# Moving the gate, merge, mLSTM-input and output-projection products of a hybrid recurrent decoder step from fp32r parts to scaled fp16 parts

## The chip, the cores and the metric

The kernel runs on one core of one Trainium2 chip. The metric is the device time of one execution in microseconds. The kernel before has a median of 1895.54 us over three runs (1894.94 to 1898.8). Engines: TensorE (PE, its weight loads shown as PEld), VectorE (DVE), ScalarE (ACT), GpSimd (POOL) and SyncE (SP), which issues most weight loads.

## The reference

One layer of a decoder trunk over 288 tokens (256 of a prompt, 8 x 4 of samples), model width 2048. With `xn = rmsnorm(x) * (1 + sc1) + sh1`:

```
proj = xn @ w_in                      # 2048 x 12320: RG-LRU, GLA, mLSTM inputs, gates
y_lru, y_gla, y_ml = three recurrent branches, each 1024 wide
gate = sigmoid(mg)                    # 3 x 2048 columns of proj
merged = gate0 * (y_lru @ w_br_lru) + gate1 * (y_gla @ w_br_gla) + gate2 * (y_ml @ w_br_ml)
x = x + gt1 * (merged @ w_out)
x = x + gt2 * (relu(norm2(x) @ w_ff1)**2 @ w_ff2)   # hidden width 8192
```

All in float32. The six shift, scale and gate vectors come from `silu(c) @ w_ada`. The branch states (a linear recurrence, a GLA state per head, an mLSTM matrix memory) are outputs too.

## The kernel before

Features lie on partitions and the 288 tokens along the free axis, so a weight tile of 128x128 is the stationary operand and a tile of 128x288 moves. A float32 product is made of three: high weight by high input, high by low, low by high, summed in one PSUM bank. The three branches, called side work below, run beside the weight streams, as generators that `run` advances by one step after each chunk of a stream. A chunk is 128x1024 weights, 512 KB, and makes 24 products.

Two kinds of stream exist. `stream` (lines 159 to 169) loads a chunk into one of three raw buffers on SyncE's queue, ScalarE rounds it to an fp32r high part (line 160), VectorE subtracts to get the low part (line 162), and line 169 multiplies. Everything ahead of the feed-forward goes through it: q, k, v and the RG-LRU input in four rounds of four k-tiles each, then the GLA gate, then for each of the three branches four pairs of a merge-gate block and a merge block (`merge`), with the mLSTM input blocks ahead of the second branch and its output gate ahead of the third, then `wout`. The branch outputs are split into fp32r parts by `split` (lines 647 and 648).

`Block` (lines 224 to 264) is the fp16 form, used by the feed-forward alone. ScalarE squares each of the four chunks of a block with an accumulated row sum (`scan`, line 236), a small product with ones adds the partitions (`total`, line 240), VectorE turns the sum into a power of two (`power_of_two`, lines 198 to 201) and `convert` writes scaled high and low fp16 parts into a pair buffer: the high part on ScalarE (line 249) or VectorE (line 251), the low part on VectorE (line 252). Line 263 multiplies. `feed_forward` scans ten chunks ahead, converts three ahead, and keeps the order of PE, ACT and DVE instructions of the stream as written (`in_order`). The order of the rest on each engine comes from the planner of the tile framework, by priorities; SyncE's order is the program's.

The conditioning products (`cond_product`, line 372, and `cond_parts`, line 433) are issued in between by a pattern of letters given to `every`.

## Time and profile before

| what | value |
|---|---|
| median of the runs | 1895.54 us |
| profiled execution | 1895.68 us |
| its span, first to last instruction | 1893.9 us |
| busy share PE / DVE / ACT / POOL | 98 / 67 / 59 / 12% |
| fp32r products (line 169) end, first fp16 product | 1084.8, 1093.8 us |
| granted TensorE clock | 0.995 |

A row of a group reads: line, engine, operation, output and inputs, shapes, count, then busy time and mean duration, then idle time ahead of it with what ended most of it. TensorE products overlap in the pipeline, so the length of one is not the distance between two. The chain of waits is read as start, length and what ran. A row of stages gives busy time and instruction count per engine.

### The profile page before, as it was taken

What the parts mean: (1) busy time and instruction counts of PE and PEld (TensorE: products, weight loads), DVE (VectorE), ACT (ScalarE), POOL (GpSimd) and SP (SyncE); (2) the same over time, 40 slices, a digit from 0 to 9 for tenths busy, and PEclk for the clock granted to TensorE, in tenths of its full rate; (3) what the DMA queues carried; (4) which work ended last, traced back from release to release, by engine and by line L of the source; (5) the groups of instructions that cost most, each with busy time, mean ns of one, the idle gap of its engine ahead of it and who ended that gap; (6) DMA issues with size and microseconds to landing.
All of it is one profiled execution on the core that took longest, in us unless ns stands there. A gap on an engine that the chain in (4) does not pass through costs nothing.

```text
span 1893.9 us, 38893 instructions
## 1 busy us (share of the span) xinstructions
PE 1847.8 (98%) x15874; PEld 1621.6 (86%) x15874; DVE 1268.2 (67%) x2239; ACT 1117.3 (59%) x1861; POOL 219.9 (12%) x302
## 2 busy tenths in 40 slices
PE   8999999999999999999999979999999999999997
PEld 7998889999999999999999947777777777777775
DVE  4767846645684557776558678776868676767676
ACT  5333374545454444566448568877777766666673
POOL 0001200000123010011101520000000000000091
PEclk9999999999999999999999999999999999999999
DMA  9998666547844358856787656565556555556541
GB/s 384 398 372 301 242 236 240 201 145 260 276 159 168 134 172 296 302 204 223 296 341 298 246 210 222 172 222 185 189 188 203 176 181 168 188 169 188 168 155 51
DMA packets 113442, 422.90 MB, mean 223 GB/s; under 512 B 11808, under 2 KB 12096, under 8 KB 110064
## 3 DMA queue, kind: packets, MB, share of 16 engines
q1 hardware_dynamic: 97040, 361.04, 54.9%
q0 software_dynamic: 11472, 42.79, 6.4%
q10 hardware_dynamic: 4752, 16.60, 2.2%
q8 instruction: 124, 2.03, 0.4%
q14 instruction: 54, 0.44, 0.1%
HBM read 403.56 MB, written 16.81 MB: 222 GB/s over the span
## 4 chain that ended last, share of the span: by engine, by line
PE 80%; DVE 9%; ACT 6%; issue 3%; DMA 1%; POOL 0%; SPq 0%; DVEq 0%; ACTq 0%; POOLq 0%
PE mm L169 39%; PE mm L263 24%; PE pi L263 6%; PE pa L372 3%; DVE pair L252 2%; ACT pair L249 2%; PE px L169 2%; DVE lo L162 1%; ACT con L236 1%; DMA raw<-win 1%; ACT hi L160 1%; PE pa L433 1%; DVE pair L251 0%; DVE s L800 0%; PE px L1649 0%
## 5 line engine op out<-in xcount | busy, mean ns | idle before, releaser
L263 PEld LDWEIGHTS <-pair 128*128 128x128 f16 x6144 | 596.6, 98 | 176.8 <-issue 11.9
L160 ACT ACTIVATE hi<-raw 128x1024 fp32r<-128x1024 f32 x272 | 286.9, 1057 | 407.4 <-PE mm L169 250.4
L162 DVE TENSOR_TENSOR lo<-raw,hi 128x1024 fp32r<-128x1024 f32 x272 | 334.9, 1233 | 248.0 <-ACT hi L160 227.9
L169 PE MATMUL mm<-xh,hi 128*128 128x288 f32 x1440 | 429.4, 301 | 4.0 <-ACT xh L718 1.7
L169 PE MATMUL mm<-xl,hi 128*128 128x288 f32 x1440 | 423.5, 297 | 0.0
L169 PE MATMUL mm<-xh,lo 128*128 128x288 f32 x1440 | 411.9, 296 | 2.0 <-DVE lo L162 1.9
L263 PE MATMUL mm<-x,pair 128*128 128x288 f16 x2448 | 316.1, 287 | 10.1 <-ACT x L1824 6.3
L263 PE MATMUL mm<-hx,pair 128*128 128x288 f16 x2472 | 321.8, 286 | 2.7 <-ACT s L1873 1.4
L169 PEld LDWEIGHTS mm<-xh,hi 128*128 128x128 f32 x1440 | 270.4, 188 | 15.8 <-issue 8.1
L169 PEld LDWEIGHTS mm<-xl,hi 128*128 128x128 f32 x1440 | 270.8, 188 | 1.4
L169 PEld LDWEIGHTS mm<-xh,lo 128*128 128x128 f32 x1440 | 266.0, 188 | 4.9 <-DVE lo L162 2.9
L169 PE MATMUL mm<-s,hi 128*128 128x288 f32 x1280 | 252.8, 297 | 1.1 <-DVE s L1769 0.7
L169 PEld LDWEIGHTS mm<-s,hi 128*128 128x128 f32 x1280 | 201.8, 188 | 5.1 <-issue 2.9
L169 PE MATMUL mm<-s,lo 128*128 128x288 f32 x640 | 179.2, 296 | 1.6 <-DVE lo L162 1.0
L252 DVE SCALAR_TENSOR_TENSOR pair<-xl,sums,pair 128x1024 f16<-128x1024 f32 x92 | 117.8, 1284 | 62.9 <-ACT pair L249 61.6
L252 DVE SCALAR_TENSOR_TENSOR pair<-s,sums,pair 128x1024 f16<-128x1024 f32 x92 | 118.1, 1284 | 52.7 <-ACT pair L249 51.4
L252 DVE SCALAR_TENSOR_TENSOR pair<-raw,sums,pair 128x1024 f16<-128x1024 f32 x72 | 93.2, 1295 | 41.6 <-ACT pair L249 40.6
L169 PEld LDWEIGHTS mm<-s,lo 128*128 128x128 f32 x640 | 116.9, 188 | 2.3 <-DVE lo L162 2.1
L1861 POOL TENSOR_SCALAR s<-s,mod 128x256 f32<-128x256 f32 x16 | 21.5, 1347 | 675.7 <-DVE s L1877 675.7
L236 ACT ACTIVATE con<-s 128x1024 bf16<-128x1024 f32 x92 | 96.3, 1046 | 1.3 <-DMA s<-wf 0.3
L236 ACT ACTIVATE con<-xl 128x1024 bf16<-128x1024 f32 x92 | 96.2, 1046 | 0.9
L263 PE MATMUL pi<-hx,pair 128*128 128x288 f16 x600 | 89.8, 286 | 3.1 <-DVE rs_t L1767 1.8
(526 smaller groups left out, 2275.7 us busy)
## 6 DMA issues: line engine op xcount, KB each, us to landing
raw<-win SPq DMA_DIRECT2D x192, 512.0 KB, 4.4
s<-wf SPq DMA_DIRECT2D x92, 512.0 KB, 3.9
xl<-wf SPq DMA_DIRECT2D x92, 512.0 KB, 4.1
raw<-wf SPq DMA_DIRECT2D x72, 512.0 KB, 3.9
s<-wq SPq DMA_DIRECT2D x20, 1024.0 KB, 8.7
raw<-wout SPq DMA_DIRECT2D x32, 512.0 KB, 5.9
s<-wada SPq DMA_DIRECT2D x13, 1024.0 KB, 7.3
ag<-wada POOLq DMA_DIRECT2D x12, 1024.0 KB, 7.8
```

The source lines that it names most:

```text
L160: pace["hi"] = S.activation(hi, raw, AF.Copy)
L162: pace["lo"] = V.tensor_tensor(out=lo, in0=raw, in1=hi.bitcast(F32), op=ALU.subtract)
L169: pace["last"] = T.matmul(ps, w[:, kk, ms], x, start=k == k0 and i == 0, stop=k == kt - 1 and i == 2)
L236: pace["hi"] = S.activation(junk, raw, AF.Square, accum_out=self.of[:, g:g + 1])
L249: pace["hi"] = S.activation(hi, raw, AF.Copy, scale=self.u)
L252: pace["lo"] = V.scalar_tensor_tensor(lo, raw, self.u, hi, ALU.mult, ALU.subtract)
L263: pace["last"] = T.matmul(self.ps[m][:, :N], a[:, kk, m * P:(m + 1) * P], x, start=k == 0 and i == 0, stop=k == 4 * self.kg - 1 and i == 2)
L372: pace["prod"] = T.matmul(ps[32 * j:32 * j + 32, h * w // 4:(h + 1) * w // 4], stat(k), v[:, j], start=k == 0 and h == 0, stop=k == kt - 1 ...
L433: pace["prod"] = T.matmul(ps[32 * j:32 * j + 32, a:a + 256], c, v[:, j], start=q == i == n == 0, stop=q == KT // each - 1 and n == 1, skip ...
L1861: G.tensor_scalar(a[:, 0:NP], a[:, 0:NP], mod[:, GT2, k, 0:1], None, ALU.mult)
```

## The change

The streams from the GLA gate to `wout` become `Block`s, in one list with the feed-forward's, fed by one pipeline (`feed`, `pipe_fetch`, `pipe_scan`, `pipe_total`, `pipe_convert`). Blocks of `win` beyond column 3072 (a new array `win2`) and of `wout` become 256 wide, four k-tiles to a chunk; merge blocks stay 512 wide. The pipeline scans eight chunks ahead and converts three ahead, with seven places for raw chunks; in the feed-forward it gets four more places and scans ten ahead. The first streams, on `stream`, stay as they are.

The normalised input is kept as fp16 parts: `shift_first` writes those of the first four k-tiles, `halve` makes the other twelve from the fp32r parts (two groups of four with sums on POOL, one with sums on DVE). Branch outputs are squared, totalled and scaled by `measured` before they are split into fp16. The factor of each merge block goes into its gate by one extra ScalarE operation per block (`pre`), and a bound for the merged sum, gathered by `weigh`, scales its fp16 parts (`halve_merged`, `merged`). The narrow products of `wsm` become fp16 and run after the eighth chunk of the gate blocks. In the `wout` stage the output is scaled through `mod` (`ev_o`). Cut to its core:

```diff
+    def rows_total(of, n, p=None):
+
+        p = misc() if p is None else p
+        T.matmul(p[:, 0:n], words(ones, 1, BF16), words(of[:, 0:n], 1, BF16), start=True, stop=True)
+        return p
...
     class Block:
 
...
         def scan(self, g, raw):
             if g == 0:
                 self.of = sc([P, 8], "sums", 4)
-            pace["hi"] = S.activation(junk, raw, AF.Square, accum_out=self.of[:, g:g + 1])
+            pace["hi"] = S.activation(pipe["junk"], raw, AF.Square, accum_out=self.of[:, g:g + 1])
 
         def total(self):
-            self.p = misc()
-            T.matmul(self.p[:, 0:4], words(ones, 1, BF16), words(self.of[:, 0:4], 1, BF16), start=True, stop=True)
+            self.p = rows_total(self.of, 4, None if pipe["now"] is None else pipe["now"].ps[-1][:, N:N + 4])
 
         def scale(self):
-            t, self.u = power_of_two(self.p, 4, self.of)
-            self.c = self.of[:, 7:8]
-            V.tensor_tensor(out=self.c, in0=t, in1=self.back(), op=ALU.mult)
+            self.t, self.u = power_of_two(self.p, 4, self.of, None if self.branch is None else self.of[:, 0:1])
+            if self.branch in pipe["sums"]:
+                self.weigh()
+
+        def weigh(self):
+            z = pipe["sums"]["z"]
+            V.scalar_tensor_tensor(z, self.of[:, 0:1], pipe["sums"][self.branch], z, ALU.mult, ALU.add)
+            self.branch = None
 
         def convert(self, g, raw, hi, lo):
             if g in self.by_act:
@@ -251,9 +262,15 @@
                 V.tensor_scalar(hi, raw, self.u, None, ALU.mult)
             pace["lo"] = V.scalar_tensor_tensor(lo, raw, self.u, hi, ALU.mult, ALU.subtract)
 
+        def start(self, act, back, factor):
+            if self.branch is not None:
+                self.weigh()
+            self.c = self.of[:, 7:8]
+            V.scalar_tensor_tensor(self.c, self.t, factor, back, ALU.mult, ALU.mult)
+            self.act = act
+            self.ps = [bank() for _ in range(self.nm_t)]
...
+    pipe = {"blocks": [], "places": [], "raws": {}, "pairs": {}, "fetched": 0, "scanned": 0, "converted": 0, "totals": 0, "at": 0,
+            "scan": 8, "total": 4, "now": None, "before": {}, "after": {}, "sums": {}}
...
+    def pipe_fetch():
+
+        while pipe["places"] and pipe["fetched"] < 4 * len(pipe["blocks"]):
+            i = pipe["fetched"]
+            b, raw = pipe["blocks"][i // 4], pipe["places"].pop(0)
+            Q.dma_start(raw, b.w[b.blk, b.g0 + i % 4])
+            pipe["raws"][i] = raw
+            pipe["fetched"] += 1
+
...
+    def pipe_convert(to):
+
+        while pipe["converted"] <= min(to, 4 * len(pipe["blocks"]) - 1):
+            i = pipe["converted"]
+            b, g = pipe["blocks"][i // 4], i % 4
+            if g == 0:
+                b.scale()
+            t = wp.tile([P, 2048], F16, tag=("hi", "lo")[i % 2], name=nm("pair"), bufs=3)
+            pipe["pairs"][i] = t[:, 0:1024], t[:, 1024:2048]
+            raw = pipe["raws"].pop(i)
+            b.convert(g, raw, *pipe["pairs"][i])
+            pipe["places"].append(raw)
+            pipe["converted"] += 1
+            pipe_fetch()
+
+    def feed(count, act, evac, back, factor=1.0, pre=None, by_k=None):
+
+        for j in range(count):
+            for g in range(4):
+                s = pipe["at"]
+                b = pipe["blocks"][s // 4]
+                with in_order():
+                    for f in pipe["before"].pop(s, ()):
+                        f()
+                    if g == 0:
+                        b.start(act, back() if callable(back) else back, factor)
+                        pipe["now"] = b if pipe["total"] == 4 else None
+                        if pre:
+                            pre(b.c)
+                    pipe_convert(s + 3)
+                    pipe_scan(s + pipe["scan"])
+                    ms, kks = range(b.nm_t), range(b.kg)
...
+                    for m in ms:
+                        if pipe["now"] and g == 0 and m == ms[-1]:
+                            pipe_total(s // 4 + 1)
...
+                        if g == 3:
+                            evac(j * b.nm_t + m, b.ps[m][:, :N], b.c)
+                    del pipe["pairs"][s]
+                    pipe_total((s + pipe["total"]) // 4)
+                    for f in pipe["after"].pop(s, ()):
+                        f()
+                pipe["at"] += 1
+                yield
...
+    def halve(g, E):
+
+        u, ts = xof[:, 6:7], []
+        for i in range(4):
+            ts.append(t288())
+            E.tensor_tensor(out=ts[i], in0=low(4 * g + i).bitcast(F32), in1=xh[g][:, i, :].bitcast(F32), op=ALU.add)
+        group16(g)
+        for i in range(4):
+            h, l = (x16[g][:, i, j] for j in range(2))
+            S.activation(h, ts[i], AF.Copy, scale=u)
+            V.scalar_tensor_tensor(l, ts[i], u, h, ALU.mult, ALU.subtract)
+
...
-        ylru.extend([slot(0, F32R), slot(1, F32R)])
+        yield from measured(ylru, hh, slot(0, F16), "lam0", 0)
+
+    z = []
+
+    def measured(y, src, dst, tag, branch):
+
+        of = sc([P, 8], tag, 1)
+        y16 = dst
+        for h in range(4):
+            S.activation(pipe["junk"][:, 0:2 * N], flat(src[:, 2 * h:2 * h + 2]), AF.Square, accum_out=of[:, h:h + 1])
+            if h == 1:
+                yield
+        yield
+        p = rows_total(of, 4)
+        yield
+        t, u = power_of_two(p, 4, of, of[:, 0:1])
+        V.tensor_scalar(of[:, 0:1], of[:, 0:1], 16.0, None, ALU.mult)
...
         for h in range(4):
             r = slice(2 * h, 2 * h + 2)
-            split(ylru[0][:, r], ylru[1][:, r], hh[:, r])
-            yield
+            S.activation(y16[:, 0, r], src[:, r], AF.Copy, scale=u)
+            V.scalar_tensor_tensor(y16[:, 1, r], src[:, r], u, y16[:, 0, r], ALU.mult, ALU.subtract)
+            if h % 2:
+                yield
+        y.extend((y16, t))
...
+    finish(halves_)
+    halve(3, V)
+
...
+    def branch_blocks(br, w):
+        for b in range(4):
+            for i in range(2):
+                pipe["blocks"].append(Block(io["win2"], 2 * (B_MG - B_GATE + 4 * br + b) + i, 256))
+            pipe["blocks"].append(Block(io[w], b, 512, branch=br))
+
+    branch_blocks(0, "wbl")
+    pipe["blocks"] += [Block(io["win2"], 2 * (B_MX - B_GATE) + i, 256) for i in range(4)]
+    branch_blocks(1, "wbg")
+    pipe["blocks"] += [Block(io["win2"], 2 * (B_MO - B_GATE) + i, 256) for i in range(4)]
+    branch_blocks(2, "wbm")
+    pipe["blocks"] += [Block(io["wout"], i, 256) for i in range(8)]
+    for hb in range(9):
+        if hb < 8:
+            pipe["blocks"] += [Block(io["wf1"], 4 * hb + i, 256, by_act=(0,)) for i in range(4)]
+        if hb:
+            pipe["blocks"] += [Block(io["wf2"], i, 512, g0=4 * (hb - 1), by_act=(0, 2, 3)) for i in range(4)]
+    xlw = [big.tile([P, n], F32, tag=f"xl{i}", name=nm("xw")) for i, n in enumerate((9 * N, 2048))]
+    pipe["junk"] = xlw[0][:, 2048:2560].bitcast(BF16)
+    raw3 = [wp.tile([P, 1024], F32, tag="raw", name=nm("raw"), bufs=3) for _ in range(3)]
+    pipe["places"] += [xlw[0][:, 0:1024], xlw[0][:, 1024:2048], *raw3, xlw[1][:, 0:1024], xlw[1][:, 1024:2048]]
...
+    with in_order():
+        pipe_fetch()
+        pipe_scan(3)
+        S.activation(pipe["junk"][:, 0:512], wn_[:, 0:512], AF.Square, accum_out=wn_of[:, 0:1])
+        pipe_total(0)
+        wp_ = rows_total(wn_of, 1)
+        pipe_convert(1)
...
+        pipe_convert(2)
+        pipe_scan(7)
...
+    def narrow():
+
+        p = longp()
         for i in range(4):
-            for n, t in enumerate((xh, xl)):
+            for n, (a, b) in enumerate(((wnh, 0), (wnh, 1), (wnl, 0))):
                 for j in range(4):
-                    T.matmul(p[32 * j:32 * j + 32, :N], wn[:, 4 * i + j, :], t[:, 4 * i + j, :].bitcast(F32),
-                             start=i == 0 and n == 0, stop=i == 3 and n == 1)
-        S.copy(sm, p[:, :N])
+                    k = 4 * i + j
+                    T.matmul(p[32 * j:32 * j + 32, :N], a[:, 32 * k:32 * k + 32], act_x(k)[b], start=i == 0 and n == 0, stop=i == 3 and n == 2)
+        S.activation(sm, p[:, :N], AF.Copy, scale=wn_of[:, 7:8])
+
     sg = slot(2)
 
...
-    run(stream(win, B_GATE, act1, KT, gate_silu(0)))
-    run(stream(win, B_GATE + 1, act1, KT, gate_silu(4)))
+    pipe["after"][7] = [narrow]
+    run(feed(4, act_x, gate_silu, back1))
...
-            run(stream(win, B_MG + 4 * br + b, act1, KT, lambda m, p: S.activation(gt[:, m, :], p, AF.Tanh, scale=0.5)))
+            run(feed(2, act_x, lambda m, p, c: S.activation(gt[:, m, :], p, AF.Tanh, scale=c), back1, 0.5))
...
-            def ev(m, p):
...
                 k = 4 * b + m
                 a = acc[k // 8][:, k % 8, :]
                 if br == 0:
-                    V.scalar_tensor_tensor(a, gt[:, m, :], 1.0, p, ALU.add, ALU.mult)
+                    V.tensor_tensor(out=a, in0=gt[:, m, :], in1=p, op=ALU.mult)
                     return
                 t = t288()
-                V.scalar_tensor_tensor(t, gt[:, m, :], 1.0, p, ALU.add, ALU.mult)
+                V.tensor_tensor(out=t, in0=gt[:, m, :], in1=p, op=ALU.mult)
                 (V if br == 1 else G).tensor_tensor(out=a, in0=a, in1=t, op=ALU.add)
-                if br == 2:
-                    h, l = mrg[k // 8][:, k % 8, :], mrg[2 + k // 8][:, k % 8, :]
-                    S.activation(h, a, AF.Copy, scale=0.5)
-                    V.scalar_tensor_tensor(l, a, 0.5, h.bitcast(F32), ALU.mult, ALU.subtract)
-
-            run(stream(w, b, lambda k: (y[0][:, k, :], y[1][:, k, :]), 8, ev))
+                if br == 2 and b == 3:
+                    halve_merged(k)
+
+            run(feed(1, lambda k: (y[0][:, 0, k, :], y[0][:, 1, k, :]), ev, lambda: y[1],
+                     pre=lambda c: S.activation(gt, gt, AF.Identity, bias=c, scale=c)))
+
+    def halve_merged(k):
+
+        m, a, u = mrg[k // 8], acc[k // 8][:, k % 8, :], z[0][:, 6:7]
+        S.activation(m[:, 0, k % 8], a, AF.Copy, scale=u)
+        V.scalar_tensor_tensor(m[:, 1, k % 8], a, u, m[:, 0, k % 8], ALU.mult, ALU.subtract)
+
+    def merged():
+
+        power_of_two(z[0][:, 0:1], 1, z[0])
+        for k in range(0, 12, 3):
+            for i in range(3):
+                halve_merged(k + i)
+            yield
...
-    for b in range(2):
-        run(stream(win, B_MX + b, act1, KT, to_slot(mx, 4 * b)))
+    run(feed(4, act_x, lambda m, p, c: S.activation(mx[:, m, :], p, AF.Copy, scale=c), back1))
...
+    finish(pipe["merged"])
+    run(feed(6, act_m, ev_o, z[0][:, 5:6], 0.5))
+    drain("sm1")
...
+    for i in range(3):
+        scaled(i)
+    run(feed(2, act_m, lambda m, p, c: ev_o(12 + m, p, c), z[0][:, 5:6], 0.5))
...
+    for hb in range(9):
+        if hb < 8:
+            run(feed(4, lambda k: (y16[k // 4][:, 0, k % 4, :], y16[k // 4][:, 1, k % 4, :]), ev_1(hb), xback, by_k=hb == 0))
+            s = pipe["at"]
+            at_ = pipe["after"]
+            hidden_rows(hb)
+            at_.setdefault(s, []).append(lambda hb=hb: hidden_total(hb))
+            for i in range(4):
+                at_.setdefault(s + 1 + 2 * i, []).append(lambda hb=hb, i=i: hidden_part(hb, i))
...
+        if hb:
+            x = hx[(hb - 1) % 2]
+            run(feed(4, lambda k, x=x: (x[:, 0, k, :], x[:, 1, k, :]), ev_2(hb - 1), lambda hb=hb: hback[hb - 1][0]))
...
```

423 lines of the change are left out of this document (199 added, 224 removed).

## The prediction

> **What bounds the kernel now.** I read the busy times first, then the chain that ended last, then the groups, then busy times by stage.
>
> ```profile
> span 1893.9 us, 38893 instructions
> PE 1847.8 (98%) x15874; PEld 1621.6 (86%) x15874; DVE 1268.2 (67%) x2239; ACT 1117.3 (59%) x1861; POOL 219.9 (12%) x302
> ...
> 861.94 41.66 PE mm L169 x312
> ...
> 1459.17 11.78 PE mm L263 x96
> ```
>
> The last two rows are pieces of the chain: start, length, what. TensorE is busy nearly throughout and the chain runs along it, so the end moves with TensorE's issue rate and with nothing else, as long as the other engines deliver. The two pieces are uninterrupted streams of the same 128x128 by 128x288 product: fp32r on line 169 takes 41.66 / 312 = 133.5 ns each, fp16 on line 263 takes 11.78 / 96 = 122.7 ns. (The groups' means below, near 300 ns, overlap and cannot be used as a rate.)
>
> **The change, part by part.** Durations are those of the profiled execution, 1895.68 us for a span of 1893.9, which is 0.14 us above the median of the runs, 1895.54. The sum is made against 1895.7.
>
> 1. The rate. Of the streams, only the q/k/v and RG-LRU blocks ahead of about 214 us stay fp32r. What moves to fp16 is 18 blocks of `win` at 192 products, 12 merge blocks at 96 and 4 blocks of `wout` at 192: 5376 products, in 224 chunks of 24. At 133.5 - 122.7 = 10.8 ns each they give 58.1 us. The number of products stays: three per weight tile, before and after.
>
> 2. What a chunk costs the other engines.
>
> ```profile
> L169 PE MATMUL mm<-xh,hi 128*128 128x288 f32 x1440 | 429.4, 301 | 4.0 <-ACT xh L718 1.7 <-DVE s L962 1.1 <-DVE s L744 0.8
> L162 DVE TENSOR_TENSOR lo<-raw,hi 128x1024 fp32r<-128x1024 f32 x272 | 334.9, 1233 | 248.0 <-ACT hi L160 227.9 <-PE pi L1632 4.7 <-PE pa L372 3.9
> L160 ACT ACTIVATE hi<-raw 128x1024 fp32r<-128x1024 f32 x272 | 286.9, 1057 | 407.4 <-PE mm L169 250.4 <-DMA raw<-win 69.2 <-issue 29.3
> L252 DVE SCALAR_TENSOR_TENSOR pair<-s,sums,pair 128x1024 f16<-128x1024 f32 x92 | 118.1, 1284 | 52.7 <-ACT pair L249 51.4
> L251 DVE TENSOR_SCALAR pair<-s,sums 128x1024 f16<-128x1024 f32 x46 | 34.5, 750 | 0.0
> L236 ACT ACTIVATE con<-s 128x1024 bf16<-128x1024 f32 x92 | 96.3, 1046 | 1.3 <-DMA s<-wf 0.3
> L236 ACT ACTIVATION_READ_ACCUMULATOR con<-s 128x1 f32 x92 | 17.2, 187 | 0.0
> L249 ACT ACTIVATE pair<-s,sums 128x1024 f16<-128x1024 f32 x46 | 52.4, 1138 | 37.4 <-DVE sums L201 31.0 <-DVE sums L200 4.1 <-DVE sums L245 2.1
> L198 DVE TENSOR_REDUCE sums<-px 128x1 f32<-128x4 f32 x64 | 10.0, 155 | 1.7 <-PE px L240 1.7
> L200 DVE TENSOR_SCALAR sums<-sums 128x1 int32<-128x1 int32 x64 | 9.8, 154 | 2.2
> L240 PE MATMUL px<-sums,ones 128*128 128x4 bf16 x64 | 10.7, 168 | 2.1 <-ACT con L236 2.1
> ```
>
> Today a chunk costs ScalarE 1.057 (the high part) and VectorE 1.233 us (the low part). Afterwards ScalarE squares it (1.046 + 0.187) and makes the high part of chunks 0 and 2 of four (1.138 / 2): 1.802, which is +0.745. VectorE makes the other high parts (0.750 / 2) and every low part (1.284): 1.659, which is +0.426. Each block adds a reduce and four small scalar operations at 0.154 to 0.155, together 0.77 us on VectorE; there are 56 (36 of `win`, now 256 wide, 12 merge, 8 `wout`). All this is hidden only while both engines keep up with TensorE, so I add it stage by stage (columns: stretch, length, busy of PE, PEld, DVE, ACT, POOL with counts, clock, DMA).
>
> ```profile
> 210.00:310.00 100.00, 98.88 (x775) 88.08 (x774) 59.44 (x96) 56.04 (x84) 9.00 (x15) 1.00 0.64 227
> 310.00:479.00 169.00, 168.85 (x1356) 157.88 (x1355) 88.84 (x126) 78.87 (x120) 14.90 (x26) 1.00 0.61 210
> 479.00:568.00 89.00, 88.36 (x704) 83.12 (x705) 66.73 (x114) 48.34 (x71) 17.97 (x28) 1.00 0.63 214
> 568.00:742.00 174.00, 174.00 (x1456) 165.78 (x1458) 94.89 (x170) 81.07 (x139) 27.24 (x50) 1.00 0.54 181
> 742.00:833.00 91.00, 91.00 (x772) 85.98 (x761) 68.56 (x138) 48.32 (x76) 3.91 (x8) 1.00 0.85 294
> 833.00:973.00 140.00, 139.09 (x1180) 134.25 (x1182) 81.73 (x115) 74.77 (x110) 21.37 (x15) 1.00 0.68 251
> 973.00:1085.00 112.00, 109.32 (x922) 105.81 (x915) 81.89 (x157) 79.15 (x123) 32.33 (x31) 1.00 0.79 300
> ...
> 1132.80:1880.00 747.20, 741.02 (x6183) 589.86 (x6182) 545.49 (x953) 536.55 (x946) 57.04 (x59) 1.00 0.55 177
> ...
> 1000.00:1050.00 50.00, 47.73 (x397) 46.05 (x398) 44.76 (x86) 43.24 (x66) 8.31 (x7) 1.00 0.73 275
> ```
>
> The stages are, in order, gates and the first merge gate; merge 0; mLSTM inputs and a gate; merge 1; the mLSTM output gate and a merge gate; merge 2; `wout`. Chunks 24, 40, 24, 40, 24, 40, 32; blocks 6, 10, 6, 10, 6, 10, 8. Each chunk saves TensorE 24 x 10.8 ns = 0.26 us. So the stages shrink to 93.8, 158.6, 82.8, 163.6, 84.8, 129.6 and 103.7 us, against VectorE demands of 74.3, 113.6, 81.6, 119.7, 83.4, 106.5 and 101.7. In the third, fifth and last stage VectorE is wanted 98% of the time, and ScalarE in the last one 79.15 + 32 x 0.745 = 103.0 us, 99%. Behind a late conversion on VectorE wait the state updates and the mLSTM's elementwise steps, and behind those TensorE itself, whose order is fixed. The nearest row for how much a loaded engine delivers is the stretch from 1000 us: VectorE at 90% with ScalarE at 86%, TensorE still 47.73 of 50. At 90% the three stages need 90.7, 92.7 and 114.4, which is 7.9 + 7.9 + 10.7 = 26.5 us over TensorE's need. The other bound is nothing: weights are squared eight chunks and converted three chunks ahead, and the neighbouring stages have room. I take 16, nearer the row.
>
> 3. Where the fp16 streams begin.
>
> ```profile
> 214.27 4.02 PE px L953 x64
> ...
> 207.83 8.79 SPq L159 DMA_DIRECT2D raw<-win  x4
> ...
> raw<-win SPq DMA_DIRECT2D x192, 512.0 KB, 4.4
> ```
>
> Before, the 64 narrow products fill TensorE until the gate streams start. Now the first block cannot be scaled until its four chunks are landed and squared. SyncE issues the corresponding four loads from 207.8 to 216.6, each waiting for a place; with a fourth place taken earlier from the freed low part I put the last landing at 216, its square at 217.3, total, scale and first high part at 220.5. The narrow products, now fp16 and later, cost some 1.5. Against 214.3 + 4.0 the loss is 220.5 + 1.5 - 218.3 = 3.7; I take 4, with 0 (loads early enough) and 10 (VectorE busy with the halves of x, 8 operations of 0.5) as bounds.
>
> 4. The branch outputs. They are now squared, totalled and scaled before they are split.
>
> ```profile
> 299.36 1.40 DVE L909 TENSOR_TENSOR_SCAN s<-s,s 128x288 f32<-128x288 f32 x2
> ...
> 309.85 0.43 PE L169 MATMUL mm<-s,hi 128*128 128x288 f32 x2
> ...
> 823.12 1.41 DVE L1049 TENSOR_TENSOR s<-s,px 128x576 f32<-128x576 f32 x2
> ...
> 833.30 0.43 PE L169 MATMUL mm<-s,hi 128*128 128x288 f32 x2
> ...
> L647 ACT ACTIVATE s<-s 128x576 fp32r<-128x576 f32 x12 | 7.7, 673 | 6.5 <-DVE s L1049 6.5
> ```
>
> From the last scan (300.8) to the first merge product there are 9.1 us, in the mLSTM branch 8.8. The new chain is four squares at 0.673 + 0.187 (3.4), the total (0.2), six small VectorE operations (0.9) and the first of four pairs (0.7 + 0.8): 6.0 idle, near 9 between queued chunk work. I take 2 us for each of these two branches, 4 in all, bounds 0 and 20 (twice 10, nothing hidden). The GLA branch has two gate blocks to spare and costs nothing.
>
> 5. Small items. 56 totals on TensorE, between 0.01 (a chain piece) and 0.168 us each, mostly overlapped: 3, bounds 1 and 9. The feed-forward stage is untouched, but its first conversions are now done before its norm:
>
> ```profile
> 1093.76 0.28 PE L263 MATMUL mm<-x,pair 128*128 128x288 f16 x1
> ...
> 1121.62 0.42 PE L263 MATMUL mm<-x,pair 128*128 128x288 f16 x2 [0.81 <-ACT pair L249]
> ```
>
> Its first block of 96 products takes 27.9 us, because the norm's VectorE steps and conversions share that engine; one conversion per step remains between them, so only the wait for the second block's scale goes: -2, bounds 0 and -8.
>
> Sum: 1895.7 - 58.1 + 16 + 4 + 4 + 3 - 2 = 1862.6, so 1863.
>
> By the Trainium skill ("SBUF — State Buffer", "Who interferes with whom") VectorE and GpSimd share a port pair under an exclusive lock, so a VectorE operation can be blocked for a whole GpSimd one. The 0.750 us of line 251 comes from a stage where POOL is busy 57 of 747 us; in the `wout` stage it is busy 32 of 112. By that rule the 16 conversions there would wait up to half a GpSimd operation of about a microsecond at three tries in ten, some 3 us, an estimate which would make the sum 1866.
>
> **The rivals.**
>
> Everything is absorbed: the three full stages run at TensorE's rate and start and branches cost nothing. Then 1895.7 - 58.1 - 2 + 3 = 1839. For it speaks the feed-forward stage, where VectorE at 73% loses nothing; against it that no stage of this trace runs VectorE above 90%.
>
> VectorE becomes the bound in the middle, and the kernel is slower. Its place is the seven stages, its price the share that VectorE can deliver between waits for ScalarE and TensorE. At 80% they take 93.8, 158.6, 102.0, 163.6, 104.3, 133.1 and 128.8 = 884.2 us against 875 now; with items 3 to 5 (+9) that is 1914. Break-even is near 84%. For it: line 162 and line 252 idle mostly behind ScalarE's high parts, and side chains hop between engines. Against it: the 90% row.
>
> Transfers come late. Places for raw weights are seven in the middle, so a load leaves two chunks ahead of its square, about 2 x 3.7 us, while it takes 4.4 at the median.
>
> ```profile
> ACT hi L160 <- DMA raw<-win: 69.2, 28, 7.5
> ```
>
> Today's waits average 69.2 / 28 = 2.5 us and the DMA share is 0.85 and 0.79 in two stages. Half such a wait on each of their 14 blocks is 17 us: 1880. Against it: ScalarE runs ahead of TensorE, so such a wait need not reach it.
>
> The rate does not come: if products between the side work's fp32 ones are held by something else than their type, items 3 to 5 remain, 1895.7 + 9 = 1905. Against it: the fp32r piece above lies in the middle and is uninterrupted.
>
> **How the numbers follow.** Forecast 0.58 (own range 1848 to 1879), absorbed 0.17, VectorE-bound 0.12, late transfers 0.10, no rate 0.03. The lower end is the sum with all bounds good, 1895.7 - 58.1 + 1 - 2 = 1836; the upper takes the bad bounds of items 2 to 4 short of all at once (16 + 4 + 4 replaced by 26.5 + 10 + 18): 1893, leaving out most of the slow cases. A measurement of this kernel can tell 0.2%, 3.8 us, from no change. Faster 0.80: nearly all of the first two and most of the late transfers; same 0.06; slower 0.14: VectorE-bound and no rate, less their edge cases.
>
> **What would show it.** Step 1: pieces of the chain on `pair` in the middle at 122 to 123 ns per product; at 133 it is wrong. Step 2: VectorE and ScalarE above 90% in the three named stages, with gaps ahead of products released by `pair` or `sums`; gaps there beyond 27 us in sum mean the slow rival, none the fast one. Step 3: TensorE idle 4 to 8 us after the last fp32r product. Step 4: gaps at the first product on `s` of the first and third merge. Step 5: the feed-forward's second block starting right behind its first. The forecast fails if the middle is as long as before although its products are faster.

## The result and the profile after

The changed kernel takes 1969.95 us (median, 1964.56 to 1974.53) against 1895.8 us for the kernel before on the same chip: a ratio of 1.0387, 95% interval 1.0355 to 1.0419. It is slower by 74 us; the forecast was 1863.

The page of the changed kernel, its profiled execution of 1967.13 us, busy times:

```profile
span 1965.0 us, 39819 instructions
PE 1831.6 (93%) x15920; PEld 1437.4 (73%) x15920; DVE 1401.1 (71%) x2717; ACT 1291.2 (66%) x2262; POOL 217.1 (11%) x310
...
PE 56%; DVE 12%; ACT 10%; DMA 6%; issue 3%; POOL 1%; ACTq 0%; DVEq 0%; SPq 0%; POOLq 0%
```

The last row is the chain that ended last, by engine. Here is the same row of the kernel before:

```profile
PE 80%; DVE 9%; ACT 6%; issue 3%; DMA 1%; POOL 0%; SPq 0%; DVEq 0%; ACTq 0%; POOLq 0%
```

TensorE fell from 98 to 93% busy, and the chain runs through VectorE, ScalarE and transfers for 28% of the span, where it was 16%. Two pieces of that chain, in merge 0 and in the mLSTM inputs (start, length, what):

```profile
484.65 7.61 PE mm L280 x62
...
528.16 7.61 PE mm L280 x62
```

7.61 / 62 = 122.7 ns: an uninterrupted fp16 stream has the rate that was forecast. Now busy times by stage (stretch, length, then busy time and count of PE, PEld, DVE, ACT, POOL, then granted clock, DMA share, GB/s), the seven stages of the prediction in order:

```profile
220.00:341.00 121.00, 97.64 (x760) 67.32 (x761) 74.14 (x145) 86.26 (x149) 9.85 (x15) 0.91 0.55 197
341.00:507.00 166.00, 163.54 (x1361) 123.25 (x1361) 112.64 (x203) 107.69 (x180) 15.94 (x26) 0.98 0.61 210
507.00:594.00 87.00, 84.25 (x717) 63.02 (x715) 72.78 (x155) 65.05 (x115) 15.48 (x24) 0.98 0.64 216
594.00:768.00 174.00, 167.92 (x1478) 132.22 (x1476) 121.46 (x257) 112.08 (x203) 31.99 (x51) 0.99 0.58 185
768.00:867.00 99.00, 89.29 (x764) 66.62 (x763) 78.50 (x179) 64.34 (x117) 4.30 (x8) 0.95 0.76 257
867.00:1009.00 142.00, 131.71 (x1164) 98.75 (x1164) 105.10 (x196) 109.12 (x179) 10.26 (x13) 0.99 0.66 233
1009.00:1154.00 145.00, 112.28 (x941) 82.39 (x940) 106.51 (x230) 97.15 (x169) 30.93 (x34) 0.90 0.68 257
```

Against the same stages of before, cut at their own first products (218 to 310, 743 to 833 and 974 to 1085 us there), the gates stage grew from 92 to 121 us, the output gate from 90 to 99 and the output projection from 111 to 145; the others moved by 3 us at most, either way, and the feed-forward stage, from its first to its last product, by 2 (785.8 to 787.9). What TensorE waited for (us in total, times, longest):

```profile
PE pi L697 <- POOL row L690: 12.7, 1, 12.7
PE mm L280 <- DVE sums L198: 11.6, 6, 3.7
PE mm L280 <- DVE ue L501: 10.8, 5, 3.4
PE mm L209 <- ACT xw L243: 10.3, 5, 6.2
...
PE px L209 <- ACT xw L1091: 6.4, 1, 6.4
```

In order: a row of squared residuals on GpSimd; VectorE's reading of a block's total (line 198); the splitting of condition weights; the Square passes (line 243), for which the total (line 209) stops TensorE; and the squares of a branch output. To count all such places I add up gaps: distances of more than 0.6 us between the starts of neighbouring TensorE instructions, less 0.12 for the product itself. From 217 us to the first feed-forward product there were 6.4 us of gaps before and there are 97.7 now. By stage: 27.5, 3.0, 2.9, 6.6, 11.1, 10.4, 36.2 (the last with the last merge block in it). The same stretch without its gaps shrank by 22 us, from 870.4 to 848.4, not by 58. Steps 1 and 5 below say where the other 36 went.

### The profile page after: what moved, and what is told of

Same layout as the page of the kernel before. It is cut to its first block, busy times and chain, and to the rows that moved or that the text cites. A ratio compares the mean times of both kernels' runs of the same rounds, so it can differ in the third digit from the quotient of the medians.

```text
span 1965.0 us, 39819 instructions
## 1 busy us (share of the span) xinstructions
PE 1831.6 (93%) x15920; PEld 1437.4 (73%) x15920; DVE 1401.1 (71%) x2717; ACT 1291.2 (66%) x2262; POOL 217.1 (11%) x310
## 4 chain that ended last, share of the span: by engine, by line
PE 56%; DVE 12%; ACT 10%; DMA 6%; issue 3%; POOL 1%; ACTq 0%; DVEq 0%; SPq 0%; POOLq 0%
PE mm L280 43%; PE pi L280 7%; DVE pair L263 4%; ACT pair L260 2%; ACT xw L243 2%; DMA xw<-win 2%; DVE pair L262 1%; DMA raw<-win 1%; PE pa L461 1%; DMA st<-wada 1%; POOL s L2027 1%; ACT uh L506 1%; DMA st<-gla 0%; PE pa L522 0%; DMA xw<-wbg 0%
## 5 line engine op out<-in xcount | busy, mean ns | idle before, releaser
L280 PEld LDWEIGHTS <-pair 128*128 128x128 f16 x11520 | 1121.0, 99 | 383.3 <-issue 67.9
L263 DVE SCALAR_TENSOR_TENSOR pair<-xw,sums,pair 128x1024 f16<-128x1024 f32 x222 | 287.0, 1295 | 96.1 <-ACT pair L260 93.0
L280 PE MATMUL mm<-y,pair 128*128 128x288 f16 x2448 | 317.0, 288 | 9.0 <-ACT y L2073 6.9
L243 ACT ACTIVATE xw<-xw 128x1024 bf16<-128x1024 f32 x222 | 232.4, 1047 | 67.4 <-DMA xw<-win 45.3
L280 PE MATMUL mm<-s,pair 128*128 128x288 f16 x1920 | 256.3, 293 | 18.1 <-DVE ue L501 8.1
L243 ACT ACTIVATE xw<-raw 128x1024 bf16<-128x1024 f32 x166 | 173.8, 1047 | 32.2 <-DMA raw<-win 21.3
L160 ACT ACTIVATE hi<-raw 128x1024 fp32r<-128x1024 f32 x48 | 50.8, 1059 | 99.3 <-DMA raw<-win 73.2
L169 PE MATMUL mm<-xh,hi 128*128 128x288 f32 x288 | 83.6, 302 | 4.4 <-DVE s L904 2.6
L169 PE MATMUL mm<-xl,hi 128*128 128x288 f32 x288 | 82.9, 298 | 0.0
L169 PE MATMUL mm<-xh,lo 128*128 128x288 f32 x288 | 75.6, 299 | 1.2 <-DVE lo L162 1.2
```

Of the source, the lines that this page charges most:

```text
L160: pace["hi"] = S.activation(hi, raw, AF.Copy)
L169: pace["last"] = T.matmul(ps, w[:, kk, ms], x, start=k == k0 and i == 0, stop=k == kt - 1 and i == 2)
L243: pace["hi"] = S.activation(pipe["junk"], raw, AF.Square, accum_out=self.of[:, g:g + 1])
L263: pace["lo"] = V.scalar_tensor_tensor(lo, raw, self.u, hi, ALU.mult, ALU.subtract)
L280: pace["last"] = T.matmul(self.ps[m][:, :N], a[:, kk, m * P:(m + 1) * P], x, start=k == 0 and i == 0, stop=k == 4 * self.kg - 1 and i == 2)
```

## The experiments

Unless it is said otherwise, an edit is made to the changed kernel, gains in us are counted from its 1970 us, and ratios are to the kernel before, run beside it. My first theory was that a few named waits held TensorE; the rival, that ScalarE and VectorE as a whole come too late, so that mending one wait uncovers the next.

### Single waits and edits

**GpSimd's passes behind the last blocks.**

```diff
-    for i in range(3):
-        scaled(i)
     run(feed(2, act_m, ...))
+    for i in range(3):
+        scaled(i)
```

> Edit to the changed kernel: GpSimd's three scaling passes over the residual (`scaled`, 20 us of GpSimd) are issued behind the last two output-projection blocks instead of ahead of them. Theory (they stand ahead of GpSimd's additions of squares, for which TensorE waits 12.7 + 3.8 us in its own order): the output-projection stage of 145 us gets 12 to 17 shorter, the norm gap of 9 us grows by at most 4, 1970 becomes 1955 to 1960. Rival (the wait is only where a late stage comes to rest, and the next late thing takes its place): less than 4 us.

Measured 1970.99 us, 1.039 (1.0374 to 1.0405). The trace voids this: the planner issued the passes ahead of the row all the same, the row came behind 16 of their instructions, at 1137.6 us, and TensorE waited 12.7 us for it as before. The move was made properly below.

**High parts of the first six blocks on VectorE.**

```diff
-Block(w, first_ + i, 256)
+Block(w, first_ + i, 256, by_act=())
```

> Edit to the changed kernel: in the first six blocks (the gate and the first merge gate) every high part is made by VectorE, none by ScalarE; this takes 12 operations of 1.14 us off ScalarE and gives VectorE 12 of 0.75. Theory (ScalarE alone is over-committed in this stage): its 121 us get 8 to 14 shorter. Rival (the stage waits for loads and for the start of the pipeline, not for ScalarE's throughput): at most 3 us.

1972.93 us, 1.0407 (1.0389 to 1.0424): no gain. The gates stage ended at 338.6 us in place of 341.0, and merge 0 took 171 in place of 166.5.

**The totals in a bank of their own**, on top of the edit above.

```diff
-            self.p = rows_total(self.of, 4, None if pipe["now"] is None else pipe["now"].ps[-1][:, N:N + 4])
+            self.p = rows_total(self.of, 4)
```

> The edit of e3_gate_hi_on_dve and one more: the total of the next block is put into a bank of its own instead of the unused columns of the bank that the running block accumulates in. Theory (each such total makes TensorE wait, 24 products later, for VectorE's reduce of it, since the bank is shared): the 11.6 us of waits for the reduce vanish and it is 8 to 12 us faster than e3_gate_hi_on_dve. Rival (VectorE is late anyway and the products wait for its pair instead): within 4 us of e3_gate_hi_on_dve.

1973.13 us, 1.040 (1.0384 to 1.0415). The 9.3 us for the reading of totals went, and the waits for Square passes rose from 8.1 to 16.2 us. So the next late thing took its place, at least in part. In the profiled execution the fp32r products ahead of the streams, which the edit doesn't touch, ended 5.6 us later than in the run before (at 222.5 against 216.9 us), and the stretch from there to the feed-forward was 5.9 us shorter (944.2 against 950.1). A smaller gain than the 8 to 12 us is therefore not excluded.

**One more place for raw chunks, used once.**

```diff
+    once = ring.tile([P, 2048], F32, tag="ag", name=nm("ag"))[:, 0:1024]
+    pipe["places"].append(once)
...
-            pipe["places"].append(raw)
+            if i != 7:
+                pipe["places"].append(raw)
```

> Edit to the changed kernel: an eighth place for a raw chunk, used once, so that the eighth load does not wait for the first conversion. Theory (TensorE waits 6.7 us at the start of the pipeline for the total of the second block, whose last chunk is loaded only after the first conversion): 4 to 7 us faster. Rival (ScalarE reaches these squares no earlier anyway): under 2 us.

1969.43 us (1966.8 to 1970.1), 1.0383 (1.0365 to 1.04): nothing.

**The condition weights not split.** The scale, high and low passes of `cond_parts` are left out as well.

```diff
-                for n, v in enumerate((h, words(w, 0, F16))):
+                for n, v in enumerate((words(w, 1, BF16), words(w, 1, BF16))):
```

> Edit to the changed kernel: the splitting of the conditioning weights (absolute sum, scale, high and low part, about 5.3 us of ScalarE and 3.8 of VectorE for each two k-tiles) is left out, and the conditioning products run on the raw words, so three of the conditioning vectors are not the reference's. Theory (the output-projection stage is bound by ScalarE and VectorE together, 94% busy over 70 us): the stage falls from 145 us to 112 to 120, of which the conversions' stalls are about 17 and the late scaling passes the rest; the total falls by 30 to 40. Rival (in-order handing back and forth between the two engines sets the pace of the stream, whatever else they do): less than 10.

1939.01 us, 1.0216 (1.0199 to 1.0233): 31 us less. The total is as expected, the place isn't: the last merge block and the projection together took 157 us in place of 168, so the stage lost 11 us and not 25 to 33, and merge 2 ahead of it lost another 11. This work stood in the kernel before as well, where it was covered.

**The branch outputs not measured.**

```diff
-        for h in range(4):
-            S.activation(pipe["junk"][:, 0:2 * N], flat(src[:, 2 * h:2 * h + 2]), AF.Square, accum_out=of[:, h:h + 1])
...
-        p = rows_total(of, 4)
...
-        t, u = power_of_two(p, 4, of, of[:, 0:1])
+        t, u = xof[:, 5:6], xof[:, 6:7]
```

> Edit to the changed kernel: the branch outputs are not squared and totalled; they are split with the factor of the normalised input, so the scale of the merge is not the intended one. Theory (the chain square, total, scale, split ends after the gate blocks do): the gap of 6.7 + 1.9 us ahead of the first merge, 2.2 ahead of the first merge of the third branch and some load on ScalarE go: 8 to 14 us. Rival (the branch itself, the recurrence on VectorE and ScalarE, ends late): under 5 us.

1956.42 us, 1.032 (1.030 to 1.034): 13.5 us less. Gaps of the gates stage fell from 27.5 to 22.7, of the output gate from 11.1 to 5.0.

**The output projection back on fp32r.** `wout` goes through `stream` again, the merged sum is split as before, and the feed-forward starts a pipeline of its own.

> One part of the change undone: the output projection runs as before on fp32r parts, with the merged sum split into fp32r, and the feed-forward starts its pipeline as before; gates, merges and mLSTM inputs stay fp16. Theory (the output projection in fp16 loses 34 us although its products are faster): 1970 becomes 1932 to 1942, the output-projection stage about 111 us long. Rival (it was late because the stages ahead of it hand over late work): the stage stays above 125 us.

1970.54 us, 1.0394 (1.037 to 1.0419): nothing in sum. From the last merge block to the feed-forward 168 became 142 us, but merge 2 grew by 20 and the output gate by 4. Gaps in the projection fell from 36.2 to 10.5, those of merge 2 rose from 10.4 to 22.4, the longest 6.3 us behind the splitting of condition weights. So the stage was not the cause by itself. Why merge 2 took over just that much was not settled.

### Does the type of the neighbours matter?

In the trace after, the first fp16 product starts 214 ns (median) after a float32 side product, where an fp32r one had started 117 ns after it. A kernel of nothing but products measured that by itself. Behind 240 products of each type alone, the side product is one float32 product, four of them, or a narrow bf16 one:

```diff
+    for kind in ("f32", "f32x4", "bf16"):
+        for r in range(10):
+            f32r(24)
+            side(kind)
+        f32r(24)
+        for r in range(10):
+            f16(24)
+            side(kind)
+        f16(24)
```

> A kernel of its own that computes none of the reference, only streams of 24 products of 128x128 by 128x288 out of one set of weights: fp32r, fp16, and both with one float32 product, four float32 products or one bf16 total of four columns after each 24. Theory (going back from a float32 product to an fp16 stream costs about 0.1 us more than going back to an fp32r stream, since the median step from the one to the other is 214 against 117 ns in the two traces): fp16 streams with a float32 product between show about 0.1 us more at the return, so 146 returns make 10 to 15 us. Rival (the longer steps are waits for the side work): the same step for both. Streams alone: 122.5 and 133.5 ns per product.

Its TensorE timeline (start, length, what):

```profile
19.97 31.86 PE L96 MATMUL mm<-xr,wr 128*128 128x288 f32 x240
51.67 29.57 PE L92 MATMUL mm<-x,w 128*128 128x288 f16 x240
80.98 9.74 PE L96 MATMUL mm<-xr,wr 128*128 128x288 f32 x72
90.56 0.65 PE L83 MATMUL px<-x,w 128*128 128x288 f32 x2
90.83 3.54 PE L96 MATMUL mm<-xr,wr 128*128 128x288 f32 x24
94.21 0.65 PE L83 MATMUL px<-x,w 128*128 128x288 f32 x2
```

From start to start, 240 fp32r products take 51.67 - 19.97 = 31.70 us (132.1 ns each), 240 fp16 ones 29.31 (122.1). A round of 24 fp32r and a side product takes 94.21 - 90.56 = 3.65, which is 0.48 more than 24 products. Among fp16 products the same round takes 3.43, 0.50 more than 24. The fp32r product only starts earlier (0.27 after the side product against 0.49) and makes it up behind. So the longer step costs nothing, and the rate is worth 10 ns wherever the stream runs.

### Who is late: the chain, ScalarE or VectorE

**Constant factors; the Square passes stay.**

```diff
         def total(self):
+            if self.fixed:
+                return
...
         def scale(self):
+            if self.fixed:
+                i = 0 if self.branch is None else 2
+                self.t, self.u = fix[:, i:i + 1], fix[:, i + 1:i + 2]
...
+                return
```

> Left out against the changed kernel: in the seven stages each weight block no longer takes its scale from its own sum of squares. The factor is a constant (1024 for the blocks of W_in and W_out, 512 for the branch weights, the values the measured sums give here), so the total on TensorE and the short VectorE steps behind it (reduce, mask, two shifts) fall away. The Square passes on ScalarE still run and their sums are read by nobody. The feed-forward stage is as it was. Chain theory (the stream waits because scan, total, factor and first conversion follow one another in program order, so that one late scan stops TensorE at the total): most of the 88 us of gaps in the seven stages goes, 1900 to 1925 us. Load theory (ScalarE is simply asked for more than it has, 1.24 us of Square pass for each 2.94 us of products on top of the conversions): the scans still fill ScalarE, the conversions come as late as before, 1955 to 1970 us. Side-work theory (the gaps belong to condition parts, branch sums and GpSimd rows): within 10 us of 1970.

1946.94 us, 1.0264 (1.0247 to 1.0281): 23 us less, so between the theories. The gaps fell only from 97.7 to about 90 us; most of the rest is time that TensorE spent at half its clock behind gaps, which fell from 24.5 to 13.6 us (step 5 below says how this is counted).

**Constant factors, no Square passes.**

```diff
         def scan(self, g, raw):
-            pace["hi"] = S.activation(pipe["junk"], raw, AF.Square, accum_out=self.of[:, g:g + 1])
+            if not self.fixed:
+                pace["hi"] = S.activation(pipe["junk"], raw, AF.Square, accum_out=self.of[:, g:g + 1])
```

> As the run with constant factors, and the Square passes of the seven stages on ScalarE are left out as well (228 passes of 1.05 us and 228 reads of their sums of 0.19 us, 282 us of ScalarE time by the trace of the changed kernel). Load theory: the gates stage falls from 121 us to about 95, the last merge and output projection from 168 to about 145, the whole to 1890 to 1925 us, and most of that is missing where the passes still run. Chain theory: the same time as where the passes still run, within 10 us. Side-work theory: above 1945 us, since the condition parts, the branch sums and the rows on GpSimd are still there.

1906.93 us, 1.0052 (1.0035 to 1.007): another 40 less, 63 in sum. The gates stage ends at 326.5 us against 341.0.

**No low parts.**

```diff
         def convert(self, g, raw, hi, lo):
-            pace["lo"] = V.scalar_tensor_tensor(lo, raw, self.u, hi, ALU.mult, ALU.subtract)
+            if self.w is io["wf1"] or self.w is io["wf2"]:
+                pace["lo"] = V.scalar_tensor_tensor(lo, raw, self.u, hi, ALU.mult, ALU.subtract)
...
         def multiply(self, g, hi, lo, ms, kks):
+            lo = lo if self.w is io["wf1"] or self.w is io["wf2"] else hi
```

> Left out against the changed kernel: the low parts of the weights in the seven stages (228 VectorE passes of 1.30 us, 294 us); the third product of each step multiplies the high part again, so the count of products stays. Scans, totals and factors stay. If VectorE's load sets the gaps: 1900 to 1930 us. If ScalarE's load or its order sets them, VectorE was only waiting too: 1950 to 1970 us.

1924.2 us, 1.0144 (1.0118 to 1.0169): 46 less, though scans, totals and their chain were all there. Both engines hold TensorE, then, and neither alone. The row of the gates stage with constant factors, the Square passes still running:

```profile
216.00:331.00 115.00, 96.25 (x757) 66.26 (x756) 74.19 (x128) 87.14 (x154) 11.20 (x16) 0.94 0.60 212
```

The rows of the gates stage and of the output projection without Square passes:

```profile
216.00:326.00 110.00, 98.50 (x781) 68.85 (x780) 74.02 (x139) 55.52 (x93) 10.11 (x16) 0.96 0.65 226
...
954.00:1105.00 151.00, 129.34 (x1170) 94.06 (x1169) 111.09 (x225) 81.65 (x138) 38.07 (x37) 0.94 0.72 272
```

and without low parts:

```profile
216.00:337.00 121.00, 99.65 (x770) 68.89 (x770) 45.20 (x134) 89.63 (x157) 10.12 (x16) 0.92 0.56 202
...
962.00:1119.00 157.00, 133.19 (x1172) 96.52 (x1171) 78.16 (x227) 110.66 (x196) 30.94 (x37) 0.92 0.71 263
```

(The last rows begin with the last merge block, 168 us long in the changed kernel.) Counted from the last fp32r product, the gates stage takes 124 us in the changed kernel and 120 without low parts, though VectorE's load falls from 74 to 45. It takes 115 without totals and factors, with ScalarE as busy as ever (87), and 107 when the Square passes go too (ScalarE 56). So half of the gain there belongs to the chain and half to ScalarE's passes; twelve high parts taken off ScalarE had brought only 2.4 us. The projection shrinks with either engine's load.

**Nothing measured.** Both edits on measuring together.

> Constant factors, no Square passes on the weights of the seven stages, and the branch outputs take the factor of the normalised input instead of one of their own (their Square passes, totals and the steps behind them left out, too). If the two savings add (each mends its own places): about 13 us below the run without the scans. If the scans are what made the branch measurement late: the same time as without the scans, within 4 us. Below 1893 us it would also be faster than the kernel before.

1893.07 us, 0.9983 (0.9972 to 0.9995): the savings add, 14 below the run without Square passes.

### What is left, and a faster kernel

**The row on GpSimd first**, now with an order that the planner keeps (`pace["row"]` is the addition of the thirteenth row):

```diff
-    for i in range(3):
-        scaled(i)
     run(feed(2, act_m, ...))
+    with tc.issue_after(pace["row"].ins):
+        for i in range(3):
+            scaled(i)
```

> Against the changed kernel: on GpSimd the addition of the thirteenth residual row's squares is issued ahead of the three long scaling passes (13 instructions, 14 us) and no longer behind them. The earlier run that was meant to do this left the order on GpSimd as it was. If TensorE's wait of 13.0 us for that row is worth its length: 1955 to 1960 us. If VectorE and ScalarE are so far behind in the output projection that the wait only covers theirs: 1965 to 1971 us.

1961.92 us, 1.0343 (1.0309 to 1.0376). The wait fell from 12.7 to 3.9 us, the median by 8, but the ranges overlap (1954.4 to 1969.0 against 1964.6 to 1974.5), and in the profiled execution, the slowest of the four, other waits had grown (gaps 95.9 us in place of 97.7). In the kernel where nothing is measured:

> The same move in the kernel with constant factors and nothing measured in the seven stages, in which TensorE waits 16.6 us at this place (1893 us). If the wait is worth its length there: 1877 to 1881 us. If the passes then make the first feed-forward block late instead: 1886 to 1893 us.

1884.25 us, 0.9924 (0.9908 to 0.9941): 9 us of a wait that fell from 16.3 to 6.6.

**All high parts on ScalarE**, on top:

```diff
+            self.by_act = (0, 1, 2, 3) if self.fixed else by_act
```

> As the run before (constant factors, nothing measured, the row first), and the high parts of all weights of the seven stages are made on ScalarE: 114 VectorE passes of 0.77 us (88 us) become ScalarE passes of 1.14 us (130 us). ScalarE was 58 us busy of 125 in the mean of those stages, VectorE 92. If VectorE's load still sets gaps: 5 to 15 us below the run before. If what is left are transfers and side products: within 3 us of it. If ScalarE becomes the late one again: above it.

1874.52 us, 0.9884 (0.9869 to 0.9899): the fastest kernel here, 1.2% below the kernel before. It takes constant factors that suit these weights; nothing guards them. Its page:

```profile
span 1875.7 us, 39017 instructions
PE 1805.8 (96%) x15861; PEld 1423.6 (76%) x15861; DVE 1289.9 (69%) x2362; ACT 1158.5 (62%) x1900; POOL 230.1 (12%) x310
```

The gaps are down to 30.5 us, the larger ones now the GpSimd row (7.0) and states that arrive late (6.9).

**One chunk in four measured**, on the run with the row first and the branches not measured:

```diff
         def scan(self, g, raw):
+            if g and self.few:
+                return
-            pace["hi"] = S.activation(pipe["junk"], raw, AF.Square, accum_out=self.of[:, g:g + 1])
+            pace["hi"] = S.activation(pipe["junk"], raw, AF.Square, scale=2.0 if self.few else 1.0, accum_out=self.of[:, g:g + 1])
```

> As the run with constant factors, nothing measured of the branch outputs and the row first, but every weight block of the seven stages takes its factor from a measured sum again, of one of its four chunks (the Square pass with a scale of 2, so that the sum stands for the four): 57 Square passes of 1.24 us (71 us) and all totals and factor steps are back. If it is the amount of Square passes that cost: within 10 us of the run with constant factors. If it is the chain of total and factor: 20 us or more above it.

1921.69 us, 1.0134 (1.0119 to 1.0149): 37 above constant factors, although three quarters of the Square passes are gone. TensorE's timeline shows one of nine waits:

```profile
560.80 0.17 PE L209 MATMUL mm<-sums,ones 128*128 128x1 bf16 x1
560.83 3.10 PE L283 MATMUL mm<-x,pair 128*128 128x288 f16 x24
567.05 4.21 PE L283 MATMUL mm<-x,pair 128*128 128x288 f16 x21 [3.12 <-DVE sums L198]
```

and VectorE's the reason:

```profile
562.90 1.26 DVE L969 SCALAR_TENSOR_TENSOR s<-s,par,s 128x254 f32<-128x254 f32 x3
564.08 1.27 DVE L266 SCALAR_TENSOR_TENSOR pair<-raw,sums,pair 128x1024 f16<-128x1024 f32 x1
565.28 1.65 DVE L969 SCALAR_TENSOR_TENSOR s<-s,par,s 128x253 f32<-128x253 f32 x4
566.85 0.14 DVE L198 TENSOR_REDUCE sums<-mm 128x1 f32<-128x1 f32 x1
```

The total of the next block stands at 560.8 in the bank of the running one. VectorE reads it 6 us later, behind a convolution's steps and a low part. Meanwhile 24 products run and the next waits for the reading: 0.14 us of work stops the stream for 3.1.

**VectorE relieved in that kernel** (all high parts on ScalarE):

> As the run that measures one chunk in four, with the high parts of all weights of the seven stages made on ScalarE (114 VectorE passes of 0.77 us become ScalarE passes of 1.14 us). If VectorE's load is what makes the reading of the totals late: 1900 to 1912 us, and the waits of TensorE for the reading of a total fall well below 15 us. If the order of the chain alone does it: 1916 to 1924 us.

1912.63 us, 1.0084 (1.0066 to 1.0101): 9 less, just outside what was expected; the waits for the reading fall to 9.6 us.

**The total read by ScalarE**, right behind its product:

```diff
         def total(self):
...
+            if self.few:
+                S.copy(self.of[:, 4:5], self.p[:, 0:1])
```

> As the run before, and the total is copied out of the running block's bank by ScalarE right after the total's product, not by a VectorE reduction at the place of the next block's first conversion. If the 15 us of waits are for VectorE's turn: 8 to 15 us below the run before. If ScalarE's turn comes as late: within 4 us of it.

1980.98 us, 1.0445 (1.0424 to 1.0466): 68 us above, against both expectations. Its waits:

```profile
PE mm L287 <- ACT sums L253: 81.5, 50, 4.6
```

and the run before it:

```profile
PE mm L284 <- DVE sums L198: 9.6, 9, 2.9
```

Every product on that bank that stands behind the reading in program order waits for it. Emitted with the next block's first conversion the reading left 24 products of grace; emitted right behind the total it leaves none, and ScalarE's turn comes up to 4.6 us later.

## Why the prediction was wrong, by its steps

**Step 1, the rate: right.** 122.7 ns in the stream, and 10.0 ns of difference in isolation against 10.8. In the kernel the mean step from one stream product to the next, at the full clock and without waits (steps below 0.2 us), fell from 133.0 to 122.7 ns; for 5376 products that makes 55.5 us, against 58.1 forecast. "No rate" falls.

**Step 2, what the engines can deliver: this failed.** The loads were right: VectorE was wanted for 680.8 us over the seven stages and was busy 671.1, ScalarE's 466.6 of before plus 224 x 0.745 make 633.5 and it was busy 641.7. The failure is the price of the load. I took the busiest row of before, 90%, for what an engine delivers in any stage, so +16 us with 26.5 as the bad bound. The gates stage now runs with ScalarE 71% busy (86.26 / 121), the output gate with VectorE at 79%, the projection at 73%, and TensorE waits in all three. In the three stages that the prediction named the gaps sum to 50 us (2.9, 11.1 and 36.2), beyond the 27 set there as the sign of the slow rival. The shares didn't even tell where: the third stage, wanted 98% on VectorE, lost 2.9 us at a share of 84%, and the gates stage, which was not named, lost 27.5. A mean share hides that the work comes in turns. These are windows of the changed kernel:

```profile
295.00:305.00 10.00, 7.47 (x46) 5.09 (x44) 3.47 (x4) 9.86 (x15) 0.00 (x0) 0.83 0.34 123
...
1050.00:1065.00 15.00, 13.15 (x141) 10.03 (x140) 13.97 (x27) 15.00 (x27) 1.91 (x2) 1.00 0.74 279
1065.00:1080.00 15.00, 13.27 (x113) 9.50 (x113) 14.56 (x31) 14.36 (x25) 1.93 (x2) 1.00 0.74 276
```

and this is the stretch behind them:

```profile
1118.00:1133.00 15.00, 2.32 (x16) 1.63 (x14) 2.43 (x5) 4.23 (x8) 14.25 (x17) 0.63 0.62 251
```

In the first ScalarE alone is full, in the next two both are, and TensorE starves; then TensorE stands for the GpSimd row, and both are nearly idle with it. Time lost in one phase isn't made up in the next. Behind the row at 90% of before stood a short chain, high part, low part, product. The new one comes back to TensorE on its way: Square on ScalarE, total on TensorE, reading and factor on VectorE, high part, low part, product. The runs price it: totals and factors 23 us, Square passes another 40, of which I had 16 for all. Also, I added ScalarE's new load only to the last stage. In the gates stage the row of before and 24 x 0.745 make 73.9 us, and it was busy 86.3. Among the rest are four chunks that are squared there ahead of the next stage (28 for 24 multiplied, 5 us), the gate's evacuation in two steps (7.4 for 3.2 us), two more table loads (2.6) and the branch's squares (3.5). This load is half of the matter there: of the 17 us that the runs got back in the gates stage, 9 came with the totals and factors and 8 with the Square passes, as shown above.

**Step 3, the start: the middle of its bounds was wrong.** The first fp16 product came at 220.2, as worked out (220.5), in part by luck: the fourth square ended at 216.2 in place of 217.3, and total, factor and first high part took 3.9 us in place of 3.2. The loss I had not foreseen came behind it. ScalarE's timeline there:

```profile
224.45 0.72 ACT L1183 ACTIVATE st<-st,sums 128x512 f16<-128x512 f32 x1 [4.32 <-DVE sums L202]
225.07 1.13 ACT L260 ACTIVATE pair<-raw,sums 128x1024 f16<-128x1024 f32 x1
226.11 1.04 ACT L243 ACTIVATE xw<-raw 128x1024 bf16<-128x1024 f32 x1
...
229.64 1.06 ACT L243 ACTIVATE xw<-xw 128x1024 bf16<-128x1024 f32 x1
```

ScalarE stood 4.3 us for the factor of the narrow weights, which VectorE makes, and squared chunks five to eight only behind it; the second block's total stopped TensorE for 6.2 us meanwhile. With that gap the term is near 10, its bad bound, where I had 4.

**Step 4, the branch outputs: 13.5 us, where I took 4 of 0 to 20.** The mechanism was the one named. At the first merge TensorE waits 6.4 us for the squares and 1.7 for the first high part.

**Step 5, the small items, where I took +3 and -2, and what no step had.** Of the 55.5 us of the rate only 22 are left in the stretch without gaps. The larger part of the difference is the clock: between 217 us and the feed-forward it was granted at half in eleven stretches, 78.5 us in all (never in the kernel before), and in 49 of these TensorE was issuing. There a step from one fp16 product to the next took 240 ns, so half of the time, 24.5 us, was lost. The remaining 9 us fit the 111 more side instructions in the stretch (1799 for 1688), mostly 59 totals and the 48 narrow products that now run in it; that assignment is argued, not measured. So the first feed-forward product comes 69.3 us later: 91.3 for gaps, 24.5 and 9 for these two, less 55.5. The prediction had no term for the clock, none for the reading of totals (11.6 us) and none for GpSimd's row (12.7 us). The feed-forward stage gained nothing.

**The rivals.** Closest was "VectorE becomes the bound", slower with 1914 at an 80% share. Its sign was right, its place in part: it priced nothing for the gates stage, which lost 27.5 us, and 19 for the third, which lost 2.9. Its engine was only half right, since ScalarE's passes were worth 40 us where VectorE had its full load, and its bound of 80% was too mild. Slower had 0.14 in all, and the range stopped at 1893 because it left most of that out. (Its lower end isn't the sum with all bounds good, as it says: with the -8 of item 5 that would be 1830.6.) "Late transfers" is not supported: an eighth place, used once at the start, changed nothing, and none of TensorE's five longest waits is for a transfer. "Absorbed" (1839) is refuted for this kernel; with nothing measured and ScalarE making the high parts, 1874.5 is what came.

The sentence on the Trainium skill ("SBUF — State Buffer", "Who interferes with whom") put 3 us on line 251, now 262. Rows of the projection stage:

```profile
L263 DVE SCALAR_TENSOR_TENSOR pair<-xw,sums,pair 128x1024 f16<-128x1024 f32 x19 | 25.9, 1365 | 5.1 <-ACT pair L260 4.9
L263 DVE SCALAR_TENSOR_TENSOR pair<-raw,sums,pair 128x1024 f16<-128x1024 f32 x13 | 18.1, 1395 | 3.5 <-ACT pair L260 3.3
L262 DVE TENSOR_SCALAR pair<-xw,sums 128x1024 f16<-128x1024 f32 x10 | 7.5, 746 | 0.0
```

Line 262 is as short as ever, 746 ns; it is the low parts, which read two inputs, that are longer than the 1.29 us of the feed-forward stage, by 19 x 0.07 + 13 x 0.10 = 2.6 us. The same section says that a VectorE instruction with two inputs in SBUF contends with a GpSimd one that reads it. The size fits; that GpSimd is the reason was not tested.

The savings from the changed kernel to the fastest one, each from a difference of two medians: totals and factors 23, Square passes 40, branch measurement 14, the GpSimd row 9, high parts from VectorE to ScalarE 10. Together 95.4 us, from 1969.95 to 1874.52; another order of the edits could share them out differently. What remains open: how much of the 40 and the 23 is load and how much order (the run with a quarter of the passes still lost 37), why merge 2 grows when the projection goes back, and the totals in a bank of their own in a kernel with room, or squares and totals made further ahead, neither of which was tried.

## What to carry to other kernels

Price a new load on helper engines by the chain it adds, not by the mean share: ask for each step which engine it visits, what is queued there ahead of it, and what TensorE has left to do meanwhile. A measured scale per weight block makes such a chain; if a constant, or a factor made long before, will do, the faster type pays (0.2% here by itself, 1.2% with the row first and the high parts on ScalarE), otherwise it can cost more than it saves. And an edit to the order of work counts only when the trace shows the new order.
